# Two narrow runs of V turned into a pair by seven half-size products, with a K run moved ahead of the pairs and half of a gate's sums moved one stage on

## The chip, the cores and the metric

The kernel runs on one NeuronCore of a Trainium2 chip. The metric is the device time of one execution in microseconds (us); several executions are timed and the median stands for the kernel. TensorE (PE) does the matmuls; its loads of the stationary operand are listed as PEld. VectorE (DVE) and ScalarE (ACT) do the elementwise work, SyncE (SP) issues nearly all DMA transfers, GpSimd (POOL) is idle. "Granted clock" is the share of TensorE's full clock.

## What is computed

A decoder trunk of two layers over 512 tokens of width 2048, all in float32. Layer A is differential attention. Then the residual stream gives keys, values and forget-gate logits once, and layer B is an attention that reads them. Each layer scales and shifts its input and gates its output by rows computed from a conditioning vector `c` (for layer B: `w_mod[1]`, 3 x 2048 columns, shift, scale, gate).

```python
def shared_kv(x, c_act, w_mod_kv, b_mod_kv, w_kv, b_f):
    mod = c_act @ w_mod_kv + b_mod_kv
    shift, scale = jnp.split(mod, 2, axis=-1)
    hk = x * (1.0 + scale[:, None]) + shift[:, None]
    kvf = hk @ w_kv                                   # 2048 -> 2048 + 2048 + 16
    k, v, zf = jnp.split(kvf, [B_WIDTH, 2 * B_WIDTH], axis=-1)
    ...
    F = jnp.cumsum(log_sigmoid(zf + b_f), axis=1)

def forgetting_attention(h, w_q, w_out, k, v, F):
    proj = h @ w_q                                    # 2048 -> 2048 q, 2048 g
    ...                                               # softmax(q k^T + F[t] - F[s], causal) v
    return (o * jax.nn.silu(g)) @ w_out

x = layer_norm(alpha * x + gate * mixer(x * (1 + scale) + shift))
```

## The kernel before

**Products.** Every float32 operand is split into a high part that TensorE takes (`hh`, `whi`) and a rest (`hl`, `wlo`), and each product is three matmuls, high by high, rest by high and high by rest (`products`, L280 to L282). A matmul takes 128 rows of the depth, 128 columns of the stationary operand and up to 512 of the moving one. One group of 16 depth tiles, 4 output banks and 3 matmuls is a *run* of 192 matmuls. With `natural` the tokens are the output rows and the weights move; else the weights' columns are the output rows.

**The stream of weights.** `WeightStream` (`ws`) holds all jobs in the order in which they are used, 8 steps of two depth tiles each. SP loads a step into one of four buffers `wst`, ACT casts it to `whi` (L180), DVE subtracts to get `wlo` (L181); `whi` and `wlo` have three buffers each, so a step can be made when PE has finished the step three before.

**The stages**, with the times of the profile: layer A to about 960 us; then the shared V and K. V's columns come in pieces: 0 to 512 (`vj[0]`, to 1013.7), two *narrow runs* of 264 columns each (`vj[3]` and `vj[4]`, columns 1536 to 2048 and the 16 forget columns behind them, to 1065.5), and the 1024 columns 512 to 1536 as the *wide pair* (`seven_products`, to 1143.3): the product of a 2 x 2 split (tokens by depth, depth by columns) with seven block products of half size in place of eight, which wants sums of blocks of the tokens (`combine(s)` makes `sums`, `su` and `sl`; `put_away` stores what leaves the buffers, `back_n` loads it again) and sums of blocks of the weights (`sums` of `PairFirst` and `PairSecond`, on DVE). The products have the names `p1`, `p2`, `p3`, `p7`, and `first`, `us`, `diff` are sums on the way out. Then come the K runs `kj[0]` to `kj[3]` (to about 1319), layer B's eight projection runs `bj[0]` to `bj[7]` with attention between them (to about 1735), and four output runs `oB` (to 1905.8), in which `z` is summed and normalized.

**The sums for the rows.** The rows that come from `c` are sums on DVE, not matmuls: `mod_stream` brings 128 x 1024 pieces of `w_mod` (`ms`, 512 KB each, three buffers) and adds piece times `cact` to `macc` (an *item*, L494). After 16 items a transpose (L580) and a reduction (L581) give `mred` or `gred`, a small product with `fours` on PE (`tr`) adds up the rest (L590), the row goes to DRAM and comes back in another shape (`fetch_rows`), and `fold(1)` turns it into the two factors with which `build_h` makes layer B's input. The gate's first half is summed with shift and scale in the K runs, its second half in `bj[0]` and `bj[1]` by `gate_stream` (buffer `gs`, which shares its place with `pT`, the transposed probabilities).

**What sets the order.** A list `pieces` and an iterator `background` are moved on by one `tick` after each burst of six matmuls; a run's `bg` says after which bursts the background moves:

```python
def tick(bg):
    if pieces:
        piece = pieces.pop(0)
        for fn in piece if isinstance(piece, list) else [piece] if piece else ():
            fn()
    for _ in range(bg):
        next(background, None)
```

The framework orders the instructions from these calls and waits by semaphore where data or a buffer demands it. Each engine, and SP's queue, takes its instructions in order.

The functions that the change touches, with the line numbers of the profile:

Of the kernel before, what the change touches and what calls it, by code (L numbers as in the profile page):

```python
# [45 lines left out]
CUT = False  # L46
LAM_INIT = 0.8 - 0.6 * math.exp(-0.0)


class Job:  # L50
# [8 lines left out]
    def load(self, nc, dst, kt, keep):  # L59
        rows = self.src[kt * P : (kt + 2) * P, :]  # L60
        off = 0
        for c, n in self.parts:
            keep(nc.sync.dma_start(dst[:, :, off : off + n], rows[:, c : c + n].rearrange("(k p) n -> p k n", p=P)))
            off += n


class PairFirst:


    width = 512  # L70
    gate = None

    def __init__(self, src, c0, c1):
        self.src, self.c0, self.c1 = src, c0, c1

    def load(self, nc, dst, kt, keep):
        n = kt // 2
# [7 lines left out]
    def sums(self, nc, n, st, after, keep):  # L85
        if n >= 4:
            nc.vector.tensor_tensor(st[:, 0, :], st[:, 1, :], st[:, 0, :], op=ALU.subtract)


class PairSecond:  # L90


    width = 512
    gate = None

    def __init__(self, src, c0, c1):
        self.src, self.cols = src, (c0, c1)

    def load(self, nc, dst, kt, keep):
        n = kt // 2  # L100
        c0 = self.cols[n % 2]
        rows = self.src[2 * (n // 2) * P : (2 * (n // 2) + 2) * P, c0 : c0 + 512]
        keep(nc.sync.dma_start(dst, rows.rearrange("(k p) n -> p k n", p=P)))

    def sums(self, nc, n, st, after, keep):
        if n % 2 == 0:
# [3 lines left out]
            keep(minus(st[:, 0, :], st[:, 1, :], other[:, 1, :]))  # L110


class WeightStream:
# [23 lines left out]

    def load(self, upto):
        while len(self.stage) < min(upto, len(self.order)):
            job, s = self.order[len(self.stage)]  # L140
            if self.paired(len(self.stage)) and len(self.stage) % 3 == 2:
                st = self.spare()
            else:
                st = self.pool.tile([P, 2, 512], F32, name="wst", tag="wst", bufs=self.STAGES)
            job.load(self.nc, st, 2 * s, self.keep)
            self.stage.append(st)

    def paired(self, n):
        return n < len(self.order) and isinstance(self.order[n][0], (PairFirst, PairSecond))
# [11 lines left out]
    def step(self, extra=None):  # L161
# [4 lines left out]
        w = job.width  # L166
        if self.paired(self.done):
            self.sums(self.done)
        if job.gate is not None:
            for k in range(2):  # L170
                self.nc.vector.tensor_tensor(st[:, k, :w], st[:, k, :w], job.gate, op=ALU.mult)
        if extra:
            hi, lo = ([extra() for _ in range(2)] for _ in range(2))
            for k in range(2):
                self.nc.scalar.copy(hi[k][:, :w], st[:, k, :w])
                self.nc.vector.tensor_tensor(lo[k][:, :w], st[:, k, :w], hi[k][:, :w].bitcast(F32), op=ALU.subtract)
        else:
            hi = self.pool.tile([P, 2, 512], F32R, name="whi", tag="whi", bufs=3)
            lo = self.pool.tile([P, 2, 512], F32R, name="wlo", tag="wlo", bufs=3)
            self.nc.scalar.copy(hi[:, :, :w], st[:, :, :w])  # L180
            self.nc.vector.tensor_tensor(lo[:, :, :w], st[:, :, :w], hi[:, :, :w].bitcast(F32), op=ALU.subtract)  # L181
            hi, lo = ([t[:, k, :] for k in range(2)] for t in (hi, lo))
# [5 lines left out]
    def cast(self):  # L188

        job, s = self.order[self.done]  # L190
        hi = self.pool.tile([P, 2, 512], F32R, name="whi", tag="whi", bufs=3)
        lo = self.pool.tile([P, 2, 512], F32R, name="wlo", tag="wlo", bufs=3)
        w = job.width
        self.nc.scalar.copy(hi[:, :, :w], self.stage[self.done][:, :, :w])
        self.done += 1
        return hi, lo, self.stage[self.done - 1], w

    def rest(self, tiles):

        hi, lo, st, w = tiles  # L200
        self.nc.vector.tensor_tensor(lo[:, :, :w], st[:, :, :w], hi[:, :, :w].bitcast(F32), op=ALU.subtract)
# [14 lines left out]
def tile_yoco(  # L216
# [40 lines left out]
    f_dram = dram.tile([B_HEADS, T], F32, name="f_dram")  # L257
    s_dram = dram.tile([4, P, TB, 512], F32, name="s_dram")
# [124 lines left out]
    vcols = [0, 512, 1024, 1536, 1800]  # L383
    vj = [Job(kv_w, [(2048 + col, 512 if col < 1536 else 264)]) for col in vcols]
# [11 lines left out]
    pair = PairFirst(kv_w, 2048 + 512, 2048 + 1024), PairSecond(kv_w, 2048 + 512, 2048 + 1024)  # L396
    for j in [o[1] for o in oA] + [vj[0], vj[3], vj[4]]:
        ws.add_job(j)
    for j, steps in zip(pair, (12, 16)):
        ws.add_job(j, steps)  # L400
    for j in kj + bj + [o[1] for o in oB]:
# [72 lines left out]
    def mod_stream(segs, new_stage, new_acc, ahead):  # L474
# [11 lines left out]
        for k, (i, kt) in enumerate(todo):  # L486
            load_upto(k if calm else k + ahead)
# [72 lines left out]
    calm = []  # L560

    def four_ones(pool):

        t = pool.tile([P, P], F32, name="fours", tag="fours")
        for k in range(0, P, 32):
            S.copy(t[k : k + 32, 0:32], ident[k : k + 32, k : k + 32])
        return t[:, 0:32]

    def mod_rows(pool, fours, dst, bias, ones_at):
# [6 lines left out]
        def steps(n, acc):  # L576
            if n == 0:
                red.append(pool.tile([P, P], F32, name="mred", tag="mred", bufs=2)[:, 0 : 16 * last])
# [358 lines left out]
    fours = four_ones(ap)  # L937
    for dst, src, col, bias, one in (
# [4 lines left out]
        steps = mod_rows(ap, fours, dst, bias[col : col + n * D], one)  # L943
# [7 lines left out]
    def vectors(pool, wanted):  # L951
        fours = four_ones(pool)
        segs = []
        for dst, src, col, bias, one in wanted:
            n = len(one)
            steps = mod_rows(pool, fours, dst, bias[col : col + n * D], one)
# [363 lines left out]
    def out_projection(jobs, layer, zp, opened, residual, norm, after_held=None):  # L1320
# [8 lines left out]

        prepare(0)  # L1330
        for k, (f, job, banks) in enumerate(jobs):
            if layer == 1:

                if k:
                    pieces.extend([None] * 8 + [lambda k=k: prepare(k + 1)])
# [3 lines left out]
            if layer == 1 and k == 2:  # L1339
                gated = ktile("gate")  # L1340
                row_bcast(gated, gate_dram[1][0, 1536:2048])
# [822 lines left out]
```

## Time and profile before

| | |
|---|---|
| median of 3 runs | 1917.32 us (1916.63 to 1917.37) |
| the profiled execution | 1917.01 us |
| its span, first to last instruction | 1915.1 us |
| PE busy | 1901.2 us (99%), 8873 matmuls |
| DVE busy | 1409.7 us (74%) |
| ACT busy | 766.3 us (40%) |
| DMA | 396.89 MB, mean 207 GB/s |
| granted clock, mean | 0.999 |

The profile is of one execution. In a timeline row stand start, duration, engine, line, operation and the tiles (out<-in); in a group's row the count, the busy time, the mean in ns, and the idle time of the engine just before with what ended it. Matmuls overlap, so the time that one takes is seen in the distance of two starts, not in its own duration. "GB/s" is what the core's 16 DMA engines moved in a stretch.

### The profile page before, as it was taken

To read this page: it belongs to the slowest core of one execution; us is meant where nothing else is said; L and a number is where in the kernel's file an instruction comes from. 1 tells how busy PE (TensorE), PEld (TensorE's weight loads), DVE (VectorE), ACT (ScalarE), POOL (GpSimd) and SP (SyncE) were. 2 spreads that over 40 slices of the span, in tenths; PEclk is the share of its full clock that TensorE was granted. 3 is DMA by queue.
4 is the path that set the end of the run, shared out by engine and by line. 5 is a ranking of instruction groups with operands and counts; after the bars stand their busy time and mean duration, and the time that the engine had idled before them with its cause. 6 is when DMAs were issued, how large, how long until landed. Compare 5 with 4: busy or idle time off the path is not lost.

```text
span 1915.1 us, 25709 instructions
## 1 busy us (share of the span) xinstructions
PE 1901.2 (99%) x8873; PEld 1584.0 (83%) x8873; DVE 1409.7 (74%) x2627; ACT 766.3 (40%) x1316; POOL 2.3 (0%) x11
## 2 busy tenths in 40 slices
PE   8999999999999999999999999999999999999998
PEld 7888888888888888888889888888888888888887
DVE  8994588777777778667676778888866666686768
ACT  3656344333333334531266632224344434453122
POOL 0000000000000000000000000000000000000000
PEclk9999999999999999999999999999999999999999
DMA  9993566676767676476656688886745555555622
GB/s 348 385 335 93 161 187 194 212 239 188 238 194 231 199 225 184 127 264 226 197 165 224 201 280 279 303 301 197 229 151 157 149 154 162 154 154 175 221 93 111
DMA packets 344594, 396.89 MB, mean 207 GB/s; under 512 B 76888, under 2 KB 255220, under 8 KB 343184
## 3 DMA queue, kind: packets, MB, share of 16 engines
q1 hardware_dynamic: 341360, 390.90, 64.1%
q10 hardware_dynamic: 3104, 4.35, 0.6%
q8 instruction: 70, 1.15, 0.2%
q14 instruction: 60, 0.49, 0.1%
HBM read 359.16 MB, written 36.00 MB: 206 GB/s over the span
## 4 chain that ended last, share of the span: by engine, by line
PE 96%; DVE 2%; DMA 1%; SPq 1%; issue 0%; ACT 0%; DVEq 0%; ACTq 0%
PE acc L280 26%; PE acc L281 26%; PE acc L282 26%; PE acc L836 4%; PE sc L836 2%; PE sc L282 2%; PE sc L281 2%; PE sc L280 2%; PE o L280 1%; PE o L282 1%; PE o L281 1%; PE o L836 1%; DMA sms<-in_w_mod_dram 1%; SPq L684 0%; PE tr L776 0%; PE tr L802 0%
## 5 line engine op out<-in xcount | busy, mean ns | idle before, releaser
L180 ACT CAST whi<-wst 128x1024 fp32r<-128x1024 f32 (+2 forms) x301 | 306.2, 1017 | 582.4 <-PE acc L282 243.2
L181 DVE TENSOR_TENSOR wlo<-wst,whi 128x1024 fp32r<-128x1024 f32 (+2 forms) x301 | 354.8, 1180 | 208.1 <-ACT whi L180 199.4
L280 PE MATMUL acc<-hh,whi 128*128 128x512 f32 x1184 | 462.9, 391 | 0.0
L281 PE MATMUL acc<-hl,whi 128*128 128x512 f32 x1184 | 462.0, 390 | 0.0
L282 PE MATMUL acc<-hh,wlo 128*128 128x512 f32 x1184 | 460.9, 390 | 0.0
L280 PE MATMUL acc<-whi,hh 128*128 128x512 f32 (+1 forms) x1008 | 381.3, 379 | 0.0
L281 PE MATMUL acc<-wlo,hh 128*128 128x512 f32 (+1 forms) x1008 | 379.6, 377 | 0.0
L282 PE MATMUL acc<-whi,hl 128*128 128x512 f32 (+1 forms) x1008 | 378.9, 376 | 0.0
L282 PEld LDWEIGHTS acc<-hh,wlo 128*128 128x128 f32 x1184 | 222.3, 188 | 47.1
L280 PEld LDWEIGHTS acc<-hh,whi 128*128 128x128 f32 x1184 | 222.4, 188 | 44.0 <-issue 0.6
L281 PEld LDWEIGHTS acc<-hl,whi 128*128 128x128 f32 x1184 | 222.5, 188 | 41.8
L282 PEld LDWEIGHTS acc<-whi,hl 128*128 128x128 f32 x1008 | 189.3, 188 | 35.2 <-DVE hl L1476 0.2
L280 PEld LDWEIGHTS acc<-whi,hh 128*128 128x128 f32 x1008 | 189.3, 188 | 33.5 <-ACT hh L275 0.3
L281 PEld LDWEIGHTS acc<-wlo,hh 128*128 128x128 f32 x1008 | 189.4, 188 | 32.3 <-DVE wlo L181 0.3
L547 DVE SCALAR_TENSOR_TENSOR macc<-ms,cact,macc 128x512 f32<-128x512 f32 x180 | 134.1, 745 | 21.1 <-DMA ms<-in_kv_w_mod_dram 13.7
L494 DVE SCALAR_TENSOR_TENSOR macc<-ms,cact,macc 128x1024 f32<-128x1024 f32 x75 | 96.1, 1281 | 23.2 <-DMA ms<-in_w_mod_dram 22.4
L734 DVE SCALAR_TENSOR_TENSOR sacc<-sms,cact,sacc 128x512 f32<-128x512 f32 (+1 forms) x128 | 90.0, 703 | 4.1 <-DMA sms<-in_w_mod_dram 0.3
L1029 ACT ACTIVATE e<-e,mn 128x128 f32<-128x128 f32 (+3 forms) x64 | 36.0, 563 | 109.6 <-DVE mn L1025 103.0
L1875 ACT ACTIVATE eb<-eb,mnb 128x128 f32<-128x128 f32 (+1 forms) x64 | 36.0, 563 | 65.7 <-DVE mnb L1872 65.0
L836 PE MATMUL acc<-wlo,hh 128*128 128x512 f32 x128 | 49.8, 398 | 0.0
L836 PE MATMUL acc<-whi,hl 128*128 128x512 f32 x128 | 49.4, 393 | 0.0
L836 PE MATMUL acc<-whi,hh 128*128 128x512 f32 x128 | 49.2, 393 | 0.0
(391 smaller groups left out, 2344.7 us busy)
## 6 DMA issues: line engine op xcount, KB each, us to landing
wst<-in_a_w_in_dram SPq DMA_DIRECT2D x240, 256.0 KB
ms<-in_w_mod_dram SPq DMA_DIRECT2D x112, 512.0 KB
ms<-in_kv_w_mod_dram SPq DMA_DIRECT2D x64, 512.0 KB
wst<-in_b_w_in_dram SPq DMA_DIRECT2D x128, 256.0 KB
wst<-in_kv_w_dram SPq DMA_DIRECT2D x59, 512.0 KB
sms<-in_w_mod_dram SPq DMA_DIRECT2D x56, 512.0 KB
wst<-in_a_w_out_dram SPq DMA_DIRECT2D x32, 512.0 KB
wst<-in_b_w_out_dram SPq DMA_DIRECT2D x32, 512.0 KB
```

The lines of the kernel that those rows point to most:

```text
L180: self.nc.scalar.copy(hi[:, :, :w], st[:, :, :w])
L181: self.nc.vector.tensor_tensor(lo[:, :, :w], st[:, :, :w], hi[:, :, :w].bitcast(F32), op=ALU.subtract)
L280: PE.matmul(dst, lhs[0], rhs[0], start=start, stop=False, skip_group_check=True)
L281: PE.matmul(dst, lhs[0], rhs[1], start=False, stop=False, skip_group_check=True)
L282: PE.matmul(dst, lhs[1], rhs[0], start=False, stop=stop, skip_group_check=True)
L494: ins = V.scalar_tensor_tensor(acc, w, one, acc, op0=ALU.mult, op1=ALU.add)
L547: ins = V.scalar_tensor_tensor(acc, w, cact[:, kt : kt + 1], acc, op0=ALU.mult, op1=ALU.add)
L734: V.scalar_tensor_tensor(acc, w, sc, acc, op0=ALU.mult, op1=ALU.add)
L836: PE.matmul(bank[n, bk], l, r, start=start, stop=stop, skip_group_check=True)
L1029: S.activation(e[:, :w], e[:, :w], AF.Exp, bias=mn, scale=-1.0, accum_out=rs)
L1875: S.activation(e[:, :w], e[:, :w], AF.Exp, bias=mn, scale=-1.0, accum_out=rs)
```

## The change

1. The two narrow runs become a pair of the same kind as the wide one, in two passes over the weights: `NarrowFirst` (6 steps of 4 depth tiles x 264 columns) and `NarrowSecond` (8 steps of 2 x 528). `seven_products` takes either pair, and stands twice in a row. Its last sums are reordered (`us` first) and use other buffers. The tiles of `wst`, `whi` and `wlo` are 1056 elements wide.
2. `kj[0]` runs right behind `v_first` (before: `vj[0]`), ahead of both pairs, with `combine(0)` to `combine(5)` and the rest of `put_away` after its steps. Its result goes to a tensor `k_dram` and comes back before `kj[3]` (`evac_k0`, `back_k`). `limit` keeps the loads of `ms` to the first 32 until the pairs are through; before, `calm` kept them from running ahead in the narrow runs and the wide pair.
3. Layer B's gate: `gate_stream(0, ...)` sums the first half of the columns in `bj[0]` and `bj[1]`, `gate_stream(1, ...)` the second half in the output runs 1 and 2, in the free half of `z`; the gates of the output runs 2 and 3 are loaded after it (`late_sums`, `late_product`, `late_gates`). Each half has a small product of its own. `mod_stream` in the K runs keeps shift and scale alone, 64 items in place of 80.
4. Pieces in the K runs stand at other ticks: `columns_of_f` 6 later, `end_of_sums`, `fetch_rows(1)` and `fold(1)` in `kj[3]`, `build_h` from its fourth step.

The core of the diff:

```diff
-    for j in [o[1] for o in oA] + [vj[0], vj[3], vj[4]]:
+    for j in [o[1] for o in oA] + [v_first, kj[0]]:
         ws.add_job(j)
-    for j, steps in zip(pair, (12, 16)):
-        ws.add_job(j, steps)
-    for j in kj + bj + [o[1] for o in oB]:
+    for pair in pairs:
+        for j, steps in zip(pair, (12, 16) if pair[0].width == 512 else (6, 8)):
+            ws.add_job(j, steps)
+    for j in kj[1:] + bj + [o[1] for o in oB]:
...
+class NarrowSecond(Pair):
+    def sums(self, nc, n, st, after, keep):
+        b11, b12, b21, b22 = self.slices(st, n)
+        minus = partial(nc.vector.tensor_tensor, op=ALU.subtract)
+        keep(minus(b12, b12, b11))
+        keep(minus(b22, b22, b12))
+        keep(minus(b11, b21, b22))
...
-            load_upto(k if calm else k + ahead)
+            load_upto(min(k + ahead, max([k, *limit[-1:]])) if limit else k + ahead)
...
+        def late_product():
+            next(background, None)
+        def late_gates():
+            gates[2] = gate_of(2)
+            jobs[3][1].gate = gate_of(3)
...
+                    if k == 2:
+                        pieces.extend([None] * 8 + [late_sums] + [None] * 6 + [late_product, late_gates])
...
+            bg = (0, lambda n: n % 5 in (1, 3), lambda n: n % 5 in (1, 3), 0)[k] if layer == 0 else [0, lambda n: n % 8 in J1, lambda n: n in J2, 0][k]
...
+        row = tiles[1][0:32, 0:32]
+        nc.sync.dma_start(row, b_mod[1][2 * D + c0 : 2 * D + c0 + 1024].rearrange("(j q) -> j q", q=32))
...
+        pt = acc_bank() if half else tr_bank()
+        PE.matmul(pt[0:32, 0:32], gred, fours, start=not half, stop=True, skip_group_check=True)
+        V.scalar_tensor_tensor(row, pt[0:32, 0:32], 0.0, row, op0=ALU.add, op1=ALU.add)
+        nc.sync.dma_start(gate_dram[1][:, c0 : c0 + 1024].rearrange("o (j q) -> (o j) q", q=32), row)
...
-    group(vj[3], True, evac_v(3), bg=lambda k: k % 16 == 7, after_sub=lambda s: combine(s // 2) if s in (1, 3, 5) else put_away(s // 2 + 1) if s in (2, 4) else None)
-    group(vj[4], True, evac_v(4), after_sub=lambda s: combine(3 + s // 2) if s in (1, 3, 5) else None)
-    seven_products()
+    group(kj[0], False, evac_k0, bg=lambda k: k % 3 == 1 and k < 30, after_sub=during_k)
+    for pair in pairs:
+        seven_products(*pair)
...
-    pieces.extend([None] * 3 + [forget_logits, None, forget_sums] + [None] * 8 + [columns_of_f])
-    for g in range(4):
-        if g == 2:
-            pieces.extend([None] * 26 + [lambda: fetch_rows(1)] + [None] * 7 + [lambda: ab.update(b=fold(1))])
+    pieces.extend([None] * 3 + [forget_logits, None, forget_sums] + [None] * 14 + [columns_of_f])
+    late = {3: (0, 1, 2, 3), 4: (4, 5, 6), 5: (7, 8, 9), 6: (10, 11), 7: (12, 13)}
+    for g in range(1, 4):
+        if g == 3:
+            back_k()
+            pieces.extend([None] * 5 + [lambda: (end_of_sums(), fetch_rows(1))] + [None] * 5 + [lambda: ab.update(b=fold(1))])
```

How the order of instructions changes is seen at three places. First DVE at the end of the sums for shift and scale, where PE takes `mred`: `ms` are the pieces of `w_mod`, `mrow` is the row that goes out. Before, in `kj[2]`:

```order
L494 SCALAR_TENSOR_TENSOR macc<-ms,cact,macc 128x1024 x2
L580 STREAM_TRANSPOSE mturn<-macc 128x512
L581 TENSOR_REDUCE mred<-mturn 128x16
L580 STREAM_TRANSPOSE mturn<-macc 128x512
L181 TENSOR_TENSOR wlo<-wst,whi 128x1024
L581 TENSOR_REDUCE mred<-mturn 128x16
L492 TENSOR_SCALAR macc<-ms,cact 128x1024
L494 SCALAR_TENSOR_TENSOR macc<-ms,cact,macc 128x1024
```

After, at the start of `kj[3]`:

```order
L559 SCALAR_TENSOR_TENSOR macc<-ms,cact,macc 128x1024
L638 STREAM_TRANSPOSE mturn<-macc 128x512
L639 TENSOR_REDUCE mred<-mturn 128x16
L638 STREAM_TRANSPOSE mturn<-macc 128x512
L639 TENSOR_REDUCE mred<-mturn 128x16
L243 TENSOR_TENSOR wlo<-wst,whi 128x1024 x2
L651 SCALAR_TENSOR_TENSOR mrow<-tr,mrow 64x32 x2
```

The items of the gate that stood behind the last reduction are gone, and the row (`mrow<-tr`) follows two steps of weights later; the place is most of a run later in the sequence of K runs.

Second SP's queue where the gate's row goes out in `bj[1]`: `tb` are transposed probabilities, `turned` their copy in DRAM, `pT` the buffer that they come back to. Before:

```order
L1309 DMA nfb<-f_dram 128x512
L1802 DMA gate_dram_79<-grow 64x32
L1888 DMA turned<-tb 128x128
L1888 DMA turned<-tb 128x256
L63 DMA wst<-in_b_w_in_dram 128x2x256
L1896 DMA pT<-turned 32x4x32 x4
L1896 DMA pT<-turned 32x4x64 x4
```

After:

```order
L2000 DMA turned<-tb 128x384
L1511 DMA gate_dram_80<-gs 32x32
L70 DMA wst<-in_b_w_in_dram 128x2x256
L2000 DMA turned<-tb 128x512
L2000 DMA turned<-tb 128x128
L2008 DMA pT<-turned 32x4x32 x4
L2008 DMA pT<-turned 32x4x64 x4
L2008 DMA pT<-turned 32x4x96 x4
L2008 DMA pT<-turned 32x4x128 x4
```

The row is now read out of `gs`, whose place `pT` takes, where `grow` was a tile of its own; more of the `turned` copies are issued ahead of it, and the 16 sends into `pT` follow in one piece.

Third DVE in the second output run of layer B: `nr` is the residual times the norm's row, `z` on the left of `cact` is `gate_stream`'s accumulator in the free half of `z`. Before:

```order
L2017 SCALAR_TENSOR_TENSOR nr<-b_16334,nr 128x512
L181 TENSOR_TENSOR wlo<-wst,whi 128x1024 x2
L2016 SCALAR_TENSOR_TENSOR nr<-nr,g_16525 128x512
L2017 SCALAR_TENSOR_TENSOR nr<-b_16526,nr 128x512
L181 TENSOR_TENSOR wlo<-wst,whi 128x1024
```

After:

```order
L243 TENSOR_TENSOR wlo<-wst,whi 128x1024
L1491 SCALAR_TENSOR_TENSOR z<-z,cact 128x1024
L2131 SCALAR_TENSOR_TENSOR nr<-nr,g_16459 128x512 x2
L2132 SCALAR_TENSOR_TENSOR nr<-b_16460,nr 128x512 x2
L243 TENSOR_TENSOR wlo<-wst,whi 128x1024
L1491 SCALAR_TENSOR_TENSOR z<-z,cact 128x1024
L2131 SCALAR_TENSOR_TENSOR nr<-nr,g_16459 128x512 x2
```

One or two items of the gate now stand between any two `wlo`, and their loads stand in SP's queue between those of `wst`.

375 lines of the change are left out of this document (218 added, 157 removed).

## The prediction, made before the changed kernel had run

> **What bounds the kernel now.** I read the page first: the shares of the engines and the chain that ended last.
>
> ```profile
> PE 1901.2 (99%) x8873; PEld 1584.0 (83%) x8873; DVE 1409.7 (74%) x2627; ACT 766.3 (40%) x1316; POOL 2.3 (0%) x11
> PE 96%; DVE 2%; DMA 1%; SPq 1%; issue 0%; ACT 0%; DVEq 0%; ACTq 0%
> ```
>
> TensorE (PE) carries 96% of the chain, so a matmul less is time less, and a wait of PE is time more. Second came PE's waits from 960 us to the end, the stretch in which the change lies; the columns are total us, times, longest.
>
> ```profile
> engine line waited for: us in total, times, longest us
> PE tr L1711 <- DVE rows L1705: 0.5, 1, 0.5
> PE sc L1482 <- ACT n L1454: 0.2, 1, 0.2
> ```
>
> So PE runs there without a break, and what has to be judged is how near the other engines come to it. Third, the stretches of the stages (busy us and instructions of each engine, granted clock, DMA share, GB/s): the two narrow runs (first two rows), part of a K run, the second output run of layer B, the densest transfers of the kernel (40 to 100 us), and the last 4 us.
>
> ```profile
> core 0: us, PE busy (x) PEld busy (x) DVE busy (x) ACT busy (x) POOL busy (x), PEclk, DMA share, GB/s
> 1013.70:1037.00 23.30, 23.30 (x172) 22.06 (x171) 15.35 (x29) 14.53 (x23) 0.00 (x0) 1.00 0.81 279
> 1037.00:1061.00 24.00, 24.00 (x203) 24.00 (x202) 14.95 (x31) 14.47 (x22) 0.00 (x0) 1.00 0.63 186
> 1230.00:1274.00 44.00, 44.00 (x197) 36.47 (x196) 33.73 (x32) 10.68 (x12) 0.00 (x0) 1.00 0.93 320
> 1778.00:1822.00 44.00, 44.00 (x196) 36.41 (x195) 30.11 (x43) 8.41 (x8) 0.00 (x0) 1.00 0.58 186
> 40.00:100.00 60.00, 60.00 (x291) 49.97 (x290) 54.98 (x76) 37.66 (x58) 0.00 (x0) 1.00 1.09 384
> 1911.00:1915.10 4.10, 0.00 (x0) 0.00 (x0) 0.13 (x1) 0.09 (x1) 0.00 (x0) 0.64 0.62 224
> ```
>
> **The matmuls.** Busy matmuls overlap, so their price is the distance of starts. These are rows of PE's timeline in the second narrow run and where the wide pair begins.
>
> ```profile
> 1061.69 0.28 PE L281 MATMUL acc<-wlo,hh 128*128 128x264 f32 x1
> ...
> 1065.40 0.28 PE L282 MATMUL acc<-whi,hl 128*128 128x264 f32 x1
> 1065.53 0.39 PE L280 MATMUL acc<-whi,hh 128*128 128x512 f32 x1
> ...
> 1143.32 0.39 PE L280 MATMUL acc<-hh,whi 128*128 128x512 f32 x1
> ...
> 1144.23 0.39 PE L281 MATMUL acc<-hl,whi 128*128 128x512 f32 x1
> ```
>
> From 1061.69 to 1065.40 there are 31 distances: 0.1197 us for a matmul of 264 columns. From 1143.32 to 1144.23 there are 4: 0.227 us for 512 columns. Two plain runs are 2 x 16 x 4 x 3 = 384 matmuls; seven products of half the depth and half the tokens are 7 x 8 x 2 x 3 = 336. The 48 that go are worth 48 x 0.1197 = **5.75 us**, whether the streaming or the weight load (busy 24.00 of 24.00 us above) sets the distance, as each takes one of both. The Trainium skill's page "TensorE: Matmul & The Clock Gate", section "Back-to-back issue gap", gives N/2.4 + 2.5 ns for a single matmul, an estimate of 112.5 ns and 5.4 us here; the rows say 119.7, and the rows decide.
>
> **Two small waits go.** The 0.5 us for the forget sums (`columns_of_f` stands 6 ticks later), and this, in PE's timeline at the wide pair's start:
>
> ```profile
> 1073.69 0.39 PE L280 MATMUL acc<-whi,hh 128*128 128x512 f32 x1
> 1073.99 0.50 PE L281 MATMUL acc<-wlo,hh 128*128 128x512 f32 x1
> 1074.32 0.39 PE L282 MATMUL acc<-whi,hl 128*128 128x512 f32 x1
> ```
>
> Distances of 0.30 and 0.33 in place of 0.227: 0.2 us lost there, where the sums of combine(6) stand ahead of a `wlo` on DVE. 0.5 + 0.2 = **0.7 us** less; bounds 0 (something else is late in their place) and 0.7.
>
> **DVE in the narrow pair.** Groups of DVE, mean ns of one behind the comma (the first three from the narrow runs, the rest from the K runs):
>
> ```profile
> L181 DVE TENSOR_TENSOR wlo<-wst,whi 128x528 fp32r<-128x528 f32 x15 | 10.5, 705 | 10.2 <-ACT whi L180 7.7 <-DMA wst<-in_kv_w_dram 2.5
> L1577 DVE TENSOR_TENSOR sums<-htmp 128x256 f32<-128x256 f32 x6 | 2.5, 424 | 2.7 <-ACT htmp L1572 2.7
> L1590 DVE TENSOR_TENSOR sl<-sums,su 128x512 fp32r<-128x512 f32 x9 | 5.7, 688 | 0.0
> L494 DVE SCALAR_TENSOR_TENSOR macc<-ms,cact,macc 128x1024 f32<-128x1024 f32 x51 | 65.4, 1282 | 22.6 <-DMA ms<-in_w_mod_dram 22.0
> L181 DVE TENSOR_TENSOR wlo<-wst,whi 128x1024 fp32r<-128x1024 f32 x33 | 40.0, 1214 | 3.8 <-ACT whi L180 3.8
> L580 DVE STREAM_TRANSPOSE mturn<-macc 128x512 f32<-128x512 f32 x6 | 4.3, 710 | 0.2
> L581 DVE TENSOR_REDUCE mred<-mturn 128x16 f32<-128x512 f32 x6 | 4.1, 683 | 0.1
> ```
>
> 14 subtractions for `wlo` of 1056 elements at 1214 x 1056/1024 = 1252 ns are 17.5 us, 4 sums of 528 at 705 ns 2.8, 24 of 264 at 424 ns 10.2, 10 in the pair's middle and end 4.2: 34.7 us in the 336 x 0.1197 = 40.2 us of the pair. That fits because the token sums (`combine`) leave this stretch for kj[0]: there 24 sums at 424 ns, 12 `sl` and 8 `wlo` and 8 items of the modulation stream make 10.2 + 8.3 + 9.7 + 10.3 = 38.5 of 43.5 us. Cost 0, covered by three buffers of `wlo`; bounds 0 and 2.4 (the 0.2 us of the wide pair's start in each of the twelve steps that have sums). DMA brings 540 KB a step there, 8 steps in 23 us or 188 GB/s, and at the worst all 4 MB of `n` come back in the same 23 us, 182 GB/s: 370, under the 384 of the 40-to-100 row. The Trainium skill's page "DMA: Bandwidth & Descriptors", section "Specifications", has a limit of about 358 GB/s of HBM for a core; by it the last of these bytes would land 23 x 12/358 = 0.8 us later (an estimate), and the sum would be up to 0.8 us less good; the row of 384 speaks against that limit here.
>
> **The moved K run.** kj[0] is the same 192 matmuls in another place. Its result makes a trip to DRAM: 4 stores of 256 KB on ACT's queue and 4 loads on SP's, which stand behind all `ms` loads and ahead of the write of `mod_dram`. They need 1 MB of transfers, 3 us at the 320 GB/s above, and nothing takes them before layer B's attention, a whole K run later; I take 0, bounds 0 and 1 (the weights behind them come later by as much as four stages of `wst` can't hide).
>
> **The sums for layer B's rows (kj[3]).** Before, the sums for shift and scale end while kj[2] runs. Timeline of DVE, its 1st and 32nd item, and PE's product:
>
> ```profile
> 1149.98 1.28 DVE L494 SCALAR_TENSOR_TENSOR macc<-ms,cact,macc 128x1024 f32<-128x1024 f32 x1
> ...
> 1231.80 1.29 DVE L494 SCALAR_TENSOR_TENSOR macc<-ms,cact,macc 128x1024 f32<-128x1024 f32 x1 [0.60 <-DMA ms<-in_w_mod_dram]
> ...
> 1256.41 0.30 PE L590 MATMUL tr<-fours,mred 128*128 128x32 f32 x2
> ```
>
> The K runs began at 1143.32, and the item at 1231.80 is the 32nd from 1149.98, that is 88.5 us in; it waited for its load, so transfers set the pace. Now 32 items are left when the pairs are through, and at this pace the last ends at 88.5 + 1.3, with two transposes and two reductions (2 x 1.39) at 92.5 us. PE reaches the product after 400 matmuls, 400 x 0.227 + 0.3 for four small ones = 91.1 us. So PE waits **1.4 us**. Bounds: none if transfers run 2% faster (fewer stores at the pair's end), 4 if 3% slower. Behind the waiting product stand all of kj[3]'s matmuls; the fold comes 6 ticks later and keeps its distance.
>
> **Layer B's gate, first half.** The product for the gate and what hangs on it before (SP's own rows are DMA issues):
>
> ```profile
> 1373.87 0.39 PE L280 MATMUL acc<-hh,whi 128*128 128x512 f32 x1
> 1374.19 0.30 PE L1800 MATMUL tr<-gfours,gred 128*64 128x32 f32 x2
> 1374.42 0.50 PE L281 MATMUL acc<-hl,whi 128*128 128x512 f32 x1
> 1375.09 1.00 SPq L1802 DMA_DIRECT2D gate_dram<-grow  x1
> 1378.94 3.74 SPq L1896 DMA_DIRECT2D pT<-turned  x8
> 1384.77 3.75 SPq L1896 DMA_DIRECT2D pT<-turned  x8
> 1397.79 0.40 PE L280 MATMUL o<-pT,vbh 128*128 128x512 f32 x1
> ```
>
> The product costs PE 0.55 less 0.227, **0.3 us**, and there will be one more of it. Before, 23.6 us pass from the product to the first `o`. Now 84 matmuls stand between, 19 us, and the 16 sends into `pT` wait until the gate's row, which lies in the same buffer, has been read out: 2 us to the write's issue, about 2 until it is done, 7.5 us for 16 issues, about 4 for landing, cast and subtraction, 15.5 in all (the 2 + 2 and the 4 are estimates from the distance of 3.85 us between the write's issue and the first send). That leaves 3 us; cost 0, bounds 0 and 3.
>
> **The gate, second half, in the output runs.** 16 items at 1282 ns are 20.5 us of DVE, 12 of them (15.4) in the second output run: 30.1 + 15.4 = 45.5 us of work in a run of 43.5. In the stage before, DVE was ahead:
>
> ```profile
> DVE wlo L181 <- ACT whi L180: 24.3, 11, 4.2
> ```
>
> From 1735 to 1865 us it waited 24.3 us for buffers of `whi` that PE gave back late, so it has a lead of about one buffer, 5 us, and 2 us of it are used up. Transfers rise from 186 GB/s by 12 x 524 KB / 43.5 us = 145 to 331, what the K runs move at 0.93. If the first items land late, `wlo` behind them does too. I take **0.5 us** (bounds 0 and 4). In the third run the last reduction stands behind the fifth `wlo`, whose buffer PE gives back after two steps, 10.9 us; with cast, subtraction, an item and 2.8 us of transposes and reductions it can be ready at 17 us, and PE takes it at 22.
>
> **Sum.** -5.75 - 0.7 + 0.3 + 1.4 + 0.5 = -4.25 us. The profiled execution took 1917.01 us (span 1915.1), so 1912.8 for it; the median of the runs is 0.3 higher, 1917.32, which gives **1913.0**.
>
> **Rivals.** *Nothing new waits* (0.23). For it: DVE and transfers kept up in every stage before, with PE's longest wait 0.5 us. Against it: the count of 32 items. -6.15 us, 1911.2. *New waits eat most of it* (0.32): kj[3] at 4 us, or the output runs at 4, or the narrow pair, with DVE at work 34.7 of 40.2 us, waiting 0.2 to 0.5 us in each step; 2.5 to 9 us of waits, 1913.6 to 1920, within 0.2%. In the same case is that the pair doesn't pay at all: PE waits for DVE there as long as it has fewer matmuls to do. *Slower* (0.12): the stream in the K runs. Its pace, 2.6 us an item from the two DVE rows above, hangs on transfers; were each of the 29 items after the first three 0.35 us slower, the reduction would come 10 us later and PE would stand for it. It decides from a wait of 10 us (6.15 + 3.8). For it speaks 0.93 of DMA time busy there, against it that the same number of weight and `ms` loads shares the queue as before. It would give 1921 to 1924. PE's clock would add to that: in the last row of the stretches PE has 4.1 us of idle time and a granted clock of 0.64. The Trainium skill's page "TensorE: Matmul & The Clock Gate", section "HAM oscillation — how this bites in real kernels", has PE slow down after some 3.4 us without work, which that row agrees with; by it a wait of 10 us would cost some us more.
>
> **How the numbers follow.** The forecast, waits of 0.7 to 2.5 us in all, has 0.33: 1911.9 to 1913.6. 0.2%, about what a measurement of this kernel can tell from no change, is 3.8 us: faster means under 1913.5. Nothing waits (0.23) and the forecast (0.33) make 0.56 for faster; the third case 0.32 for within 0.2%; slower 0.12. The range reaches from the full gain less half a us (1910.7) to 1919.0, where some 0.14 lie above and 0.05 below.
>
> **What would show it.** Right: 336 matmuls of 264 columns, 0.12 apart, 40.2 us; PE's waits list the `tr` product from `mred` with 1 to 2 us, `tr L1711` and the gap at the wide pair's start gone; no `wlo` wait over 1 us in the output runs. Wrong: a wait in the list over 4 us, distances over 0.13 us in the pair, or a granted clock under 0.99 in kj[3].

## The result and the profile after

The changed kernel takes 1944.23 us (median of 4 runs, 1943.78 to 1945.72), the kernel before 1917.34 in the runs beside it: the ratio is 1.0141 (95% interval 1.0124 to 1.0159), 26.9 us slower where 1913.0 was forecast. The profiled execution has a span of 1942.1 us at a granted clock of 0.999.

The page's shares and chain after, to be held against the two lines that open the prediction:

```profile
PE 1925.2 (99%) x8827; PEld 1581.7 (81%) x8827; DVE 1432.8 (74%) x2665; ACT 768.6 (40%) x1304; POOL 2.3 (0%) x11
PE 93%; DVE 3%; DMA 2%; SPq 1%; issue 0%; ACT 0%; ACTq 0%; DVEq 0%
```

PE has 46 matmuls fewer (48 in the pair, and two more for the gate's second product) and is 24.0 us longer busy (1925.2 against 1901.2). Its idle time in the span grew by 3 us alone (16.9 against 13.9). So most of the time was not lost in waits. PE's waits from 960 us to the end (total us, times, longest) say the same; 3.3 us in all:

```profile
PE tr L1822 <- ACT fcols L1731: 1.9, 2, 1.1
PE p L343 <- DVE wlo L243: 0.9, 1, 0.9
PE p L342 <- ACT whi L242: 0.3, 1, 0.3
PE acc L342 <- DVE htmp L1762: 0.2, 1, 0.2
```

The 0.5 us of `tr L1711` is gone, but the transposes of the forget logits now wait for ACT's copies into `fcols`; the forecast wait for `mred` is not there. Where the time went is seen in a stretch that the change doesn't touch, layer A from 500 to 700 us (busy us and instructions of each engine, granted clock, DMA share, GB/s), first of before, then of after:

```profile
500.00:700.00 200.00, 200.00 (x921) 166.89 (x920) 149.70 (x304) 71.40 (x132) 0.00 (x0) 1.00 0.70 215
```

```profile
500.00:700.00 200.00, 200.00 (x907) 164.37 (x906) 145.89 (x297) 70.86 (x130) 0.00 (x0) 1.00 0.69 214
```

At a full clock and with PE busy all the time, 907 matmuls instead of 921 fit into 200 us, 1.5% fewer. The two rows of PE's timeline that are 15 matmuls apart, in the last K run (`kj[3]`), first before, then after:

```profile
1299.70 0.39 PE L282 MATMUL acc<-hh,wlo 128*128 128x512 f32 x1
...
1303.10 0.39 PE L282 MATMUL acc<-hh,wlo 128*128 128x512 f32 x1
```

```profile
1299.61 0.40 PE L344 MATMUL acc<-hh,wlo 128*128 128x512 f32 x1
...
1303.08 0.40 PE L344 MATMUL acc<-hh,wlo 128*128 128x512 f32 x1
```

3.40 / 15 = 0.2267 us before, 3.47 / 15 = 0.2313 after. The 512-wide matmuls became 4 to 5 ns longer, in places far apart that the change leaves as they were or only moves. Over the whole profile the distances between two 512-wide matmuls (some 7374, those with a wait left out) have a mean of 232.6 ns in place of 228.9, and their sum grew by 28 us. What the change does to all of them is in the first item of the change: the tiles of `wst`, `whi` and `wlo` are 1056 elements wide, 4224 bytes in place of 4096. Tiles of a pool lie one behind the other. Before, all the tiles of weights began at 512 modulo 2048, all on a multiple of 256 bytes; after, the three of `whi` begin at 1024, 1152 and 1280, the three of `wlo` at 1408, 1536 and 1664 (addresses of the built programs). Three of the six lie 128 bytes off a multiple of 256.

### The profile page after: what moved, and what is told of

Same layout as the page of the kernel before. It is cut to its first block, busy times and chain, and to the rows that moved or that the text cites. A ratio compares the mean times of both kernels' runs of the same rounds, so it can differ in the third digit from the quotient of the medians.

```text
span 1942.1 us, 25642 instructions
## 1 busy us (share of the span) xinstructions
PE 1925.2 (99%) x8827; PEld 1581.7 (81%) x8827; DVE 1432.8 (74%) x2665; ACT 768.6 (40%) x1304; POOL 2.3 (0%) x11
## 4 chain that ended last, share of the span: by engine, by line
PE 93%; DVE 3%; DMA 2%; SPq 1%; issue 0%; ACT 0%; ACTq 0%; DVEq 0%
PE acc L343 25%; PE acc L344 25%; PE acc L342 25%; PE acc L894 4%; PE sc L894 2%; PE sc L342 2%; PE sc L344 2%; PE sc L343 2%; PE o L342 1%; PE o L344 1%; PE o L343 1%; PE o L894 1%; SPq L742 1%; DVE wlo L243 1%; DMA v_dram<-vfirst 0%
## 5 line engine op out<-in xcount | busy, mean ns | idle before, releaser
L243 DVE TENSOR_TENSOR wlo<-wst,whi 128x1024 fp32r<-128x1024 f32 (+2 forms) x299 | 361.4, 1210 | 215.3 <-ACT whi L242 212.9
L344 PE MATMUL acc<-hh,wlo 128*128 128x512 f32 x1184 | 469.1, 396 | 0.0
L343 PE MATMUL acc<-hl,whi 128*128 128x512 f32 x1184 | 468.1, 395 | 0.0
L342 PE MATMUL acc<-whi,hh 128*128 128x512 f32 (+1 forms) x912 | 358.1, 393 | 0.2 <-DVE htmp L1762 0.2
L343 PE MATMUL acc<-wlo,hh 128*128 128x512 f32 (+1 forms) x912 | 355.2, 389 | 0.0
L344 PE MATMUL acc<-whi,hl 128*128 128x512 f32 (+1 forms) x912 | 353.7, 388 | 0.0
L344 PEld LDWEIGHTS acc<-whi,hl 128*128 128x128 f32 x912 | 171.1, 188 | 39.3 <-DVE hl L1585 0.2
L342 PEld LDWEIGHTS acc<-whi,hh 128*128 128x128 f32 x912 | 171.3, 188 | 37.5 <-DVE htmp L1762 0.6
L343 PEld LDWEIGHTS acc<-wlo,hh 128*128 128x128 f32 x912 | 171.5, 188 | 34.4
L559 DVE SCALAR_TENSOR_TENSOR macc<-ms,cact,macc 128x1024 f32<-128x1024 f32 x60 | 76.8, 1281 | 13.0 <-DMA ms<-in_w_mod_dram 12.5
```

Of the source, the lines that this page charges most:

```text
L243: self.nc.vector.tensor_tensor(lo, st, hi.bitcast(F32), op=ALU.subtract)
L342: PE.matmul(dst, lhs[0], rhs[0], start=start, stop=False, skip_group_check=True)
L343: PE.matmul(dst, lhs[0], rhs[1], start=False, stop=False, skip_group_check=True)
L344: PE.matmul(dst, lhs[1], rhs[0], start=False, stop=stop, skip_group_check=True)
L559: ins = V.scalar_tensor_tensor(acc, w, one, acc, op0=ALU.mult, op1=ALU.add)
```

## Experiments

The theory behind all that follows: a matmul whose operand in SBUF starts off a multiple of 256 bytes is slower. The rivals: contention or order, or the size of a tile as such.

**The kernel before, only moved.** Two kernels in which an unused tile of 128 bytes (`b_pad128`) or 256 bytes (`b_pad256`, with 64 for 32) moves the tiles of weights and all tiles behind them:

```diff
+    gap = ctx.enter_context(tc.tile_pool(name="gap", bufs=1))
+    gap.tile([P, 32], F32, name="gap")
     wpool = ctx.enter_context(tc.tile_pool(name="wpool", bufs=2))
```

> The kernel before with 128 unused bytes per partition ahead of the weight tiles, so that wst, whi and wlo start 128 bytes off a multiple of 256 and nothing else of the program is changed. Theory A (a matmul is slower when an operand's tile starts off a multiple of 256 bytes): the 512-column matmuls are 229 to 235 ns apart in place of 227, some 20 to 28 us in all, 1937 to 1945 us. Theory B (the changed kernel is slow by its new order, its sums and transfers): no change, 1917 us.

> The same with 256 unused bytes. Theory A with a period of 256 bytes: no change, 1917 us, distances of 227 ns. Theory A with a longer period, or with the distance to the other operand's tile (hh, which stays): slow as with 128 bytes, 1937 to 1945 us. Theory B: no change.

With 128 bytes: 1958.84 us, ratio 1.021 (1.0195 to 1.0225), 40.7 us slower than the 1918.13 beside it, and more than the changed kernel. With 256 bytes: 1918.30, ratio 1.0003 (0.9994 to 1.0012). So the start of a tile modulo 256 bytes costs by itself: both programs have the instructions of the kernel before, in the same order, and differ in addresses alone. That `b_pad128` costs more than the change fits: there all tiles of weights are off, not half of them. The stretch of layer A again, in `b_pad128`:

```profile
500.00:700.00 200.00, 200.00 (x905) 164.03 (x904) 146.01 (x294) 65.23 (x119) 0.00 (x0) 1.00 0.67 212
```

Each matmul's distance to the next can be put beside the two addresses (modulo 256) of its operands, where the next has the same; medians and means in ns, for 512 columns, in `b_pad128`:

```
moving 0,   stationary 128: 3653 distances, median 232, mean 233.4
moving 128, stationary 0:   3327 distances, median 232, mean 233.9
moving 0,   stationary 0:    133 distances, median 227
moving 128, stationary 128:   79 distances, median 233
```

It makes no difference which of the two is off, and that both are off by the same amount doesn't help: each address counts, not their distance. Between aligned 512-wide matmuls of the kernel before the median is 227 and the mean 228.9. Summed over all 512-wide matmuls the distances of `b_pad128` are 35 us longer, of 42.3 us by which its span is longer; most of the rest, some 5 us, are longer waits of PE, nearly all in the first 100 us. There the transfers got slower as well:

```profile
40.00:100.00 60.00, 57.73 (x276) 46.35 (x275) 50.52 (x70) 34.60 (x52) 0.00 (x0) 1.00 1.10 350
```

The prediction shows this stretch of the kernel before with 384 GB/s at nearly the same DMA share (1.09). `b_pad64`, below, has 349, `b_pad256` 384. The gap also moves the buffers that these transfers fill (`sms`, `xt`); which of them costs this was not tried. In the changed kernel and in `a_pair`, below, `sms` and `xt` start on a multiple of 256 and the rate is 384, so nothing of it is seen in the change. ACT's casts and DVE's subtractions on the moved tiles took as long as before (1049 against 1051 ns, 1221 against 1221).

**By 64 bytes.**

```diff
+    gap.tile([P, 16], F32, name="gap")
```

> The kernel before with 64 unused bytes ahead of the weight tiles: all of them at 64 bytes off a multiple of 256. Theory, any start off a multiple of 256 costs alike: about the 1958.8 us of 128 bytes. Rival, what counts is a step of 64 bytes (only 128 off is bad): 1917 to 1919. Between the two, 1930 to 1950, if the cost goes by the share of a row that straddles a boundary.

1952.23 us, ratio 1.0177 (1.0163 to 1.0191): 34.3 us over its before (1917.92), a little less than for 128 bytes. It lies just above the middle range of what was expected and nearer to the theory. The two operands differ here, though: with the stationary operand 64 bytes off the median distance is 233 ns, with the moving one 229 (3653 and 3134 distances).

**The changed kernel with its tiles aligned.** So that no more memory is used, both parts of a step share one tile of 2112 elements, 8448 bytes, 33 x 256; the low part begins at element 1088, in the narrow pair at 1056.

```diff
+    def both(self, job, s):
+        t = self.pool.tile([P, 2112], F32R, name="wb", tag="wb", bufs=3)
+        lo = 1056 if isinstance(job, (NarrowFirst, NarrowSecond)) else 1088
+        return job.view(t, s), job.view(t[:, lo:], s)
...
-            hi, lo = (job.view(self.tile(name, F32R, 3), s) for name in ("whi", "wlo"))
+            hi, lo = self.both(job, s)
```

> The changed kernel with whi and wlo of a step in one tile of 2112 elements, the second half at element 1088 (4352 bytes) for all but the narrow pair: each starts on a multiple of 256 bytes, and the memory used is the same. Theory A: the 512-column distances are back at 227 ns, and the time is the one before less 5.75 us for 48 matmuls, less 0.5, with the 4 us of new waits that the changed kernel's list of waits shows at the narrow pair: 1915 us (1913 to 1918). Theory B: 1940 us or more.

1919.26 us, ratio 1.0008 (0.9999 to 1.0018): 25.0 us less than the changed kernel, and distances of 227 ns. The time is above the 1913 to 1918 that were expected: the new waits cost more. The stretch of layer A has 921 matmuls, as before:

```profile
500.00:700.00 200.00, 200.00 (x921) 166.75 (x920) 149.21 (x305) 72.22 (x133) 0.00 (x0) 1.00 0.68 214
```

The rest of the change, without the start of its tiles, is level with the kernel before. `wst`, which PE doesn't read, is still 1056 wide here, two of its four tiles 128 bytes off. The counterpart is the same kernel with the low part 128 bytes off in every run:

```diff
-        lo = 1056 if isinstance(job, (NarrowFirst, NarrowSecond)) else 1088
-        return job.view(t, s), job.view(t[:, lo:], s)
+        return job.view(t, s), job.view(t[:, 1056:], s)
```

> Same program as a_pair, but the low part of a step begins 4224 bytes into the shared tile in every run, so that it lies 128 bytes off a multiple of 256; tiles, buffers, sizes and order are those of a_pair. Theory (a matmul whose operand starts off a multiple of 256 bytes goes slower): a third of the 512-wide products read the low part; a third of the 40.7 us of b_pad128, where all weights were off, is 13.6, two thirds, if the matmul ahead of it is slowed as well, 27: 1932 to 1946 us, distances of 230 to 235 ns around the products of the low part. Rival (what a_pair gave back came from one tile and one release instead of two, not from where it lies): stays at 1917 to 1921, distances 227 ns.

1945.27 us, ratio 1.0141 (1.0126 to 1.0157), the changed kernel's time again, 26.0 us over `a_pair`: the upper end of what was expected. The stretch of layer A:

```profile
500.00:700.00 200.00, 200.00 (x908) 164.81 (x907) 145.07 (x296) 71.26 (x131) 0.00 (x0) 1.00 0.68 213
```

Tiles, releases and order are those of `a_pair`; so neither the one tile nor its release gave the time back, but where the low part lies. A third of the products reads the low part; 40.7 / 3 would be 13.6, so the matmul beside such a one loses too. The distances in `a_pair_off` have it: from an aligned matmul to one with the low part the median is 232 ns, and from that to an aligned one 232 to 234. Between the two aligned ones of a step it is 227 where the weights are the stationary operand, and 232 where they are the moving one: there all three lose.

**What kept the aligned kernel from its gain.** PE's waits of `a_pair` from 960 us on:

```profile
PE tr L1827 <- ACT fcols L1736: 1.9, 2, 0.9
PE tr L653 <- DVE mred L644: 1.1, 1, 1.1
...
PE p L348 <- DVE wb L248: 0.3, 1, 0.3
...
```

and the timeline of PE at the first:

```profile
1189.45 0.38 PE L1827 MATMUL tr<-ident,fcols 128*16 128x128 f32 x2
1190.78 0.28 PE L1827 MATMUL tr<-ident,fcols 128*16 128x128 f32 x1 [0.94 <-ACT fcols L1736]
1191.98 0.31 PE L1827 MATMUL tr<-ident,fcols 128*16 128x128 f32 x1 [0.93 <-ACT fcols L1736]
1192.02 0.70 PE L347 MATMUL acc<-hh,wb 128*128 128x512 f32 x1
1192.52 0.63 PE L348 MATMUL acc<-hl,wb 128*128 128x512 f32 x1
...
1195.08 0.60 PE L348 MATMUL acc<-hl,wb 128*128 128x512 f32 x1
1195.50 0.41 PE L349 MATMUL acc<-hh,wb 128*128 128x512 f32 x1
```

The copies into `fcols` stand on ACT's queue behind the stores of the sums that they are cut from. After the wait come eight matmuls 0.42 to 0.50 us apart; the stretch has a granted clock of 0.51:

```profile
1192.00:1195.50 3.50, 3.50 (x9) 2.73 (x10) 2.31 (x3) 0.88 (x1) 0.00 (x0) 0.51 0.96 330
```

So the 2.2 us of that wait (by the distances of starts) brought 1.7 us more (3.48 for eight matmuls in place of 1.81). With 1.3 us for `mred` and 0.8 in the middle of the narrow pair, by distances too, it is 6.0 us, as much as the gain that was forecast from the matmuls and the two small waits. The first remedy, the copy ahead of the store:

```diff
-            nc.scalar.dma_start(v_dram[b * P : (b + 1) * P, col : col + n], t[:, :n])
             if n < w:
                 S.copy(fcols[:, b, :], t[:, n:w])
                 fz["cols", b] = fcols[:, b, :]
+            nc.scalar.dma_start(v_dram[b * P : (b + 1) * P, col : col + n], t[:, :n])
```

> As a_pair, with the copy of the forget columns on ACT ahead of the store of the same tile, where it stood behind it. If PE's wait for fcols comes from ACT's queue standing at the store's issue, 2.3 us go: 1913 us. If it comes from DVE's sums, nothing changes against a_pair.

1919.85 us, ratio 1.0013 (1.0004 to 1.0023): no gain. The wait shrank, and two others took its place in the K runs:

```profile
PE acc L349 <- DVE wb L248: 2.5, 3, 1.6
PE tr L653 <- DVE mred L644: 1.6, 1, 1.6
PE tr L1827 <- ACT fcols L1735: 0.4, 1, 0.4
```

What the low part of the weights stands behind on DVE are the items of `w_mod`, and DVE's list for the same stretch has 15.3 us of waits for their loads:

```profile
DVE macc L564 <- DMA ms<-in_w_mod_dram: 15.3, 14, 2.3
```

That makes them the likely reason, but does not show it: in `a_pair` these waits were 14.4 us, and 22.0 in the kernel before, and in neither did PE wait for the low part in the K runs.

The next step spread these items more evenly, and took their end later; `a_late_n` also makes the tile of statistics 512 bytes wide, so that the token sums behind it are aligned:

```diff
-    pieces.extend([None] * 3 + [forget_logits, None, forget_sums] + [None] * 14 + [columns_of_f])
+    pieces.extend([None] * 5 + [forget_logits, None, forget_sums] + [None] * 14 + [columns_of_f])
...
-            pieces.extend([None] * 5 + [lambda: (end_of_sums(), fetch_rows(1))] + [None] * 5 + [lambda: ab.update(b=fold(1))])
+            pieces.extend([None] * 8 + [lambda: (end_of_sums(), fetch_rows(1))] + [None] * 5 + [lambda: ab.update(b=fold(1))])
...
-            kj[g], False, evac_k(g), bg=lambda k, g=g: (k % 2 or k % 8 == 0) if g < 3 or k < 5 else 0,
+            kj[g], False, evac_k(g), bg=lambda k, g=g: (k % 2 or k == 0) if g < 3 or k < 8 else 0,
```

> a_pair_copy with the items of layer B's stream of modulation spread more evenly in kj[1] and kj[2] (17 ticks of 32 instead of 20), the product of mred and the fold three ticks (4.1 us) later in kj[3], and the forget sums' transposes two ticks (2.7 us) later. Theory: what the change still lost once the tiles were aligned are waits for the K runs' stream (2.5 us for wb, 1.6 to 2.0 for mred, 0.6 for fcols): 4.5 to 5.5 us less than a_pair_copy, 1914 to 1915.5 us, PE's waits in kj[1] to kj[3] under 1 us in all. Rival: transfers set the end of the stream wherever its pieces are placed, and the wait moves on to the fold or to the first steps of layer B: 1917 to 1920.

> a_late with the tile of statistics 512 instead of 384 bytes wide, so that the tiles behind it (n, and the high token sums of both pairs in their buffers) begin on a multiple of 256 bytes. Theory: 192 of the 512-wide matmuls of the wide pair read those sums, at 232 to 235 ns in the kernel before; at 227 they save 1 to 1.5 us: 1913 to 1914.5. Rival: no difference to a_late within 0.3 us, if the sums' start has no part in it.

1918.76 us, ratio 1.0007 (0.9998 to 1.0016), and 1918.72 (0.9997 to 1.0014). Both theories missed; the times lie where the rivals had them. In the K runs PE waits no more, but the wait moved on, though not to the fold: to the end of `bj[0]`. PE's list, and DVE's timeline there, of `a_late`:

```profile
PE acc L347 <- DVE ql L1936: 2.7, 1, 2.7
```

```profile
1357.84 1.28 DVE L1496 SCALAR_TENSOR_TENSOR gs<-gs,cact 128x1024 f32<-128x1024 f32 x1 [0.16 <-DMA gs<-in_w_mod_dram]
1359.78 1.29 DVE L1496 SCALAR_TENSOR_TENSOR gs<-gs,cact 128x1024 f32<-128x1024 f32 x1 [0.66 <-DMA gs<-in_w_mod_dram]
1360.98 1.22 DVE L248 TENSOR_TENSOR wb<-wst,wb 128x1024 fp32r<-128x1024 f32 x1
1362.12 1.28 DVE L1936 SCALAR_TENSOR_TENSOR ql<-acc,qh 128x512 fp32r<-128x512 f32 x2
```

`ql` is read out of the bank that PE wants next, and stands on DVE behind items of the gate's stream, each paced by its load. In `a_late_n` the products of the token sums in the wide pair are 227 ns apart instead of 232 to 240 (medians), but the medians of the two kernels differ by 0.04 us: no effect that these runs can tell, since each kernel's runs scatter over more than 6 us. Two of the 16 items, then four, were moved from the end of `bj[0]` into `bj[1]`:

```diff
-            bj[p], False, evac_b(p), bg=0 if p > 1 else (lambda k: k < 4 or k == 9) if p else (lambda k: k % 2),
+            bj[p], False, evac_b(p), bg=0 if p > 1 else (lambda k: k < 6 or k == 9) if p else (lambda k: k % 2 and k < 28),
```

> a_late with the last two items of layer B's gate stream (16 items, loads from w_mod) taken from the end of bj[0] into the first ticks of bj[1], so that they no longer stand on DVE ahead of ql, whose reading frees the bank that PE waited 2.8 us for at 1359.8 us in a_late. Theory: that wait goes and nothing else is late: 2.8 us less in the span, 1912 to 1913 in the profiled execution, median 1915.5 to 1916.5 us. Rival: from the pairs' end transfers set the pace of DVE's streams, and the wait moves on once more, to the gate's product and the sends into pT in bj[1] (1 to 3 us there): 1917.5 to 1919.5.

> a_late2 with the 512-byte tile of statistics (n and the high token sums on multiples of 256 bytes; their products in the wide pair at 227 instead of 232 to 240 ns). Theory: 1 to 1.5 us less than a_late2, as the distances say: 1914 to 1915.5 us. Rival: DVE and transfers set the wide pair's pace anyway and the difference to a_late2 stays under 0.5 us.

1919.07 us, ratio 1.001 (1.0001 to 1.0018), and 1918.78 (0.9992 to 1.001). Both theories missed: the wait stayed at its place and was 4.8 us in the profiled execution of `a_late2`, so the rival's number came true without its mechanism; that the alignment gave under 0.5 us is what the rival of `a_late2_n` said. The 13th and 14th item still stood ahead of `ql`. After that wait the clock fell again:

```profile
1360.00:1364.90 4.90, 0.10 (x1) 0.00 (x0) 3.77 (x5) 1.53 (x2) 0.00 (x0) 0.97 0.95 326
1364.90:1367.90 3.00, 2.98 (x7) 2.40 (x8) 3.00 (x5) 0.00 (x0) 0.00 (x0) 0.50 0.89 296
```

With twelve items ahead of it (`k % 2 and k < 24` in `bj[0]`, `k < 8 or k == 9` in `bj[1]`):

> a_late2_n with four of the 16 gate items (not two) in bj[1] in place of bj[0]. In a_late2 the two reads into ql still stood on DVE behind the 13th and 14th item, each of them paced by its load (one in 2.4 us), and PE waited 4.8 us at 1359.7 us. Theory: with twelve items ahead of it ql comes at 1359, as ACT delivers qh by 1357.4, and the wait goes; the span falls by 3 to 5 us, median 1913 to 1916 us. Rival: DVE meets the four late items in the middle of the first attention steps of bj[1], and PE waits there for scores, weights or the sends into pT by as much: 1917 to 1920.

1915.54 us (1913.44 to 1917.11), ratio 0.9988 (0.9979 to 0.9998): the one version that is faster than the kernel before, by 2.1 us, within what was expected. PE's longest waits from 960 us on:

```profile
PE p L348 <- DVE wb L248: 0.9, 1, 0.9
PE sc L2236 <- ACT rows L2234: 0.3, 1, 0.3
PE acc L347 <- DVE ql L1936: 0.2, 1, 0.2
```

Its runs scatter over 3.7 us, those of `a_late2_n` over 9.5 (1914.09 to 1923.62); that the wait at `ql`, with or without a fall of the clock, makes the difference is what the profiles say: matched matmul by matmul, PE loses 2.5 us more at this place in `a_late` than in `a_late3_n`, 4.3 in `a_late_n`, 6.0 in `a_late2` and 4.5 in `a_late2_n`. For the runs without a profile it is not shown. In the profile of `a_late3_n` PE comes out of layer A 2.9 us later than before (first matmul behind it at 982.4 against 979.5 us), mostly from a wait near 337 us for `ah` and `al` (1.7 and 0.8 us). These waits vary between the profiles of kernels that are alike there (`ah` 0.5 us in `a_late2`, none in `a_late`), and what brings them was not tried. From the end of layer A to the end `a_late3_n` takes 4.3 us less than the kernel before (931.3 against 935.6).

## Why the prediction was wrong

**The step that failed** is not a term that was mis-sized but one that the sum hasn't got. The list of changes has the tiles "1056 elements wide", and the part on DVE in the narrow pair even prices the subtraction by 1056/1024; what the width does to where the tiles lie, and that to every matmul that reads them, stood in no term, no rival and no bound. By `a_pair` against the changed kernel it is 25.0 us, by `a_pair_off` against `a_pair` 26.0, where the changed kernel came out 31.2 us over the forecast of 1913.0. The other 6.3 us (1919.26 against 1913.0) are for the most part waits that the sum had smaller or not at all, below, and in the profile of `a_pair` 1.6 us by which PE comes later out of layer A (981.1 against 979.5). The sum itself has a slip of 0.1 us: 1912.8 + 0.3 is 1913.1. The trace of before could have given the price. In its wide pair the token sums `su` lie 128 bytes off a multiple of 256, and PE's timeline has, where their products begin:

```profile
1117.68 0.39 PE L280 MATMUL acc<-whi,hh 128*128 128x512 f32 x1
1117.91 0.39 PE L281 MATMUL acc<-wlo,hh 128*128 128x512 f32 x1
1118.13 0.40 PE L282 MATMUL acc<-whi,hl 128*128 128x512 f32 x1
1118.37 0.41 PE L280 MATMUL acc<-whi,su 128*128 128x512 f32 x1
1118.61 0.40 PE L281 MATMUL acc<-wlo,su 128*128 128x512 f32 x1
1118.85 0.39 PE L282 MATMUL acc<-whi,sl 128*128 128x512 f32 x1
```

The distances go from 0.22 to 0.24 us with the matmul ahead of the first `su`; the 192 distances in that pair with `su` on one side or both have medians of 232 to 235 ns, the 143 others 227. In `a_late_n`, where `su` is aligned, they are 226 to 227. The prediction took 0.227 from the K run behind the pair and did not ask why rows of the pair were longer. Its three signs of being wrong (a wait over 4 us, distances over 0.13 us in the narrow pair, a clock under 0.99 in `kj[3]`) all stayed away in the changed kernel: they looked only where the change was thought to act.

**The matmuls, -5.75 us.** Right in kind. The narrow pair in `a_pair`, 30 distances from the first row to the last:

```profile
1165.79 0.29 PE L347 MATMUL sc<-wb,su 128*128 128x264 f32 x1
...
1169.44 0.28 PE L347 MATMUL p<-wb,hh 128*128 128x264 f32 x1
```

3.65 / 30 = 0.1217 us where 0.1197 was taken: 384 x 0.1197 - 336 x 0.1217 = 5.1 us.

**The waits.** `mred`, forecast at 1.4 us: 1.1 in the list of `a_pair` (1.3 by the distance of the matmuls), so place and size were right in this kernel. The changed kernel has none, but that its PE is slower does not explain it: `a_pair_off`, as slow, waits longer.

```profile
PE tr L652 <- DVE mred L643: 1.6, 1, 1.6
```

Transfers against PE's pace, as it was put, is thus not shown to be the whole of it. The two small waits went (0.7 us), but what came in their place went past the bound, which had no gain at all as its worse end: 1.9 us for `fcols` (2.2 by distances, and 1.7 more at the lower clock), from a queue (ACT's, with stores ahead of copies) that the prediction had not gone through for the narrow pair's new end. In the narrow pair, taken at nothing with a bound of 2.4 us, 0.8 us were lost. The output runs, taken at 0.5 us, cost nothing that PE's list shows. The gate's second product, taken at 0.3 us, costs 0.4 by its distances in `a_pair`.

**The rivals.** "New waits eat most of it" (0.32) is what the change does once its tiles are aligned: 1919.26 us in its range of 1913.6 to 1920, though with `fcols` first among the waits, which it didn't name. "Slower" (0.12) got the direction right by luck: it had another mechanism, a late stream, and that was late by 1 to 2 us, not 10. Its side condition, that PE's clock falls after a wait, was seen at a shorter wait than the 3.4 us of the Trainium skill's page "TensorE: Matmul & The Clock Gate", section "HAM oscillation — how this bites in real kernels": in `a_pair` after 2.2 us, broken by two transposes, the clock was 0.51 for 3.5 us; in the changed kernel the same wait, and in `a_late` one of 2.7 us, were followed by a full clock (stretches right behind the waits, first of the changed kernel, then of `a_late`):

```profile
1208.00:1211.50 3.50, 3.50 (x17) 2.83 (x16) 2.39 (x3) 0.65 (x1) 0.00 (x0) 1.00 0.94 315
```

```profile
1362.80:1366.00 3.20, 3.14 (x14) 2.56 (x15) 3.20 (x6) 0.00 (x0) 0.00 (x0) 1.00 1.02 334
```

In `a_late_n`, after 2.9 us, the clock stayed at 1.00 for 0.8 us and was 0.51 for the 3.3 us behind that. What decides it is open.

## What to carry to other kernels

A tile that grows can move every tile behind it in memory: work out where the operands of the matmuls begin, modulo 256 bytes, before and after, as one asks which buffers a change lengthens. When PE is busy without a break and yet later, compare distances of starts and the count of matmuls in a stretch that the change doesn't touch. And where transfers set the pace of streams on an engine, taking away one wait lets PE reach the next one sooner: the gain is only kept when the stream's items leave the place ahead of whatever PE waits for.

## What the runs showed of the hardware

A 512-wide matmul of these types (fp32r operands in SBUF) starts 227 ns (median) after the last one when all operands begin on a multiple of 256 bytes. In `b_pad128`, `a_pair_off` and the `su` products of the kernel before it starts 232 to 235 ns after it when its own or its neighbour's moving or stationary operand begins 128 bytes off. With 64 bytes it is 233 for the stationary operand and 229 for the moving one (`b_pad64`). The granted clock was 1.00 in the stretches from 500 to 700 us that show this, and PE was busy throughout. ACT's and DVE's instructions on the same tiles took as long as before. With all buffers behind the gap 128 or 64 bytes off, transfers moved 350 and 349 GB/s from 40 to 100 us in place of 384. After waits of PE of 2.2 to 4.8 us the clock fell to half for about 3 us in `a_pair`, `a_late_n` and `a_late2`, and did not fall after 2.2 us in the changed kernel and 2.7 in `a_late`.
